# Global attention computes its scores twice, the second time keys-first, so that the probabilities are never transposed

## The chip, the cores and the metric

The kernel runs on one core of one Trainium2 chip. The metric is the device time of one launch in microseconds; of several runs the median is taken. The core has the engines TensorE (matmuls; the profile calls it PE, and its weight loads PEld), VectorE (DVE), ScalarE (ACT), GpSimd (POOL) and SyncE (SP), which here issues the DMAs.

## The reference

One layer of a hybrid backbone over 1024 latent tokens and 256 context tokens, width 1024: a modulated norm, three token mixers side by side (windowed attention, global attention, a bidirectional recurrence), their gated merge, and a gated feed-forward network. The change concerns the global attention alone. Eight query heads of 64 share two key heads; each query reads all 256 + 1024 keys:

```python
def dense_attn(q, k, v, sink=None):
    ...
    s = jnp.einsum('bqkgd,bjkd->bkgqj', q.reshape(B_, Lq, KV, G, hd), k).astype(jnp.float32) * hd ** -0.5
    ...
    p = jax.nn.softmax(s, axis=-1)[..., :k.shape[1]].astype(v.dtype)
    return jnp.einsum('bkgqj,bjkd->bqkgd', p, v).reshape(B_, Lq, HQ * hd)

def global_attn(q, k, v, ck, cv):
    ...
    k_all = jnp.concatenate([ck, k], axis=1)
    v_all = jnp.concatenate([cv, v], axis=1)
    qb = jnp.moveaxis(q.reshape(B_, nb, BLOCK, HQ, hd), 1, 0)
    o = lax.map(lambda qblk: dense_attn(qblk, k_all, v_all), qb)
```

Everything is float32. The queries and keys of this branch are normalised with large gains, so the scores need their maximum taken away before the exponential.

## The kernel before

The kernel goes through its stages in order: modulation and context, the recurrence (about 90 to 430 us of the profile), token-major projections of both attentions, windowed attention (`br` 0), global attention (`br` 1, about 889 to 1221 us), merge, output projection, feed-forward network. Most products are made from split operands: each operand is rounded into a high part (type `F32R`), the rest is kept as a low part, and a product is two or three passes of `F32R` matmuls.

A framework orders the instructions of each engine ahead of time from dependences, priorities and its own cost model, places the semaphores, and gives out buffers. The order of the program text, which is the priority, comes from `weave`: it draws from several generators in turn, in proportion to given weights. In the attention stages three are woven: the scores of iteration `it + 1`, the values of iteration `it`, and filler, which is the gate projection (`gate_unit`: eight steps of three matmuls 512 wide for one accumulator). 32 filler steps (`FILL0`) run beside the preparation, the other 80 of the global stage over 15 of its 16 iterations. An iteration is one tile of 128 tokens and one group of four heads (`it` = 2 x tile + group).

Before the change both attentions run through `attention`. `prep` loads keys and values two blocks of 128 at a time, splits them, and transposes the keys into `KH` (the high part, twice, one copy under the other: 128 rows) and `KL` (the low part, twice). `qprep` loads, scales and splits the queries and transposes them into `QT`, whose 128 rows are the high part (64) and the low part (64) of one head. So one matmul with `KH` gives high x high plus low x high, and one with `KL` the rest.

`softmax_global` (L1415 on) makes, with `QT` of one head as the stationary operand, the scores of 128 queries by 256 context keys for four heads at once (`sbc`), and by 1024 latent keys for one head at a time (`sbl`, two halves of 512). VectorE takes the maxima straight from the accumulator banks, ScalarE makes the exponentials with the maximum as its bias and sums them (`pc`, `plat`). The probabilities lie with queries on the partitions. `values` (L1303 on) turns them, four 128 x 128 transposes for each of the ten key blocks (`pp`, L1321), ScalarE rounds the result to `ph` (L1325), VectorE subtracts to `pl` (L1326), and two matmuls with the values `VHL` (64 high and 64 low columns) as stationary operand accumulate the transposed output `po` for all four heads, 512 wide (L1307, L1308). The value matmuls follow their transposes by two blocks (`PV_LAG`). The reciprocal sums are spread by GpSimd (L1450), turned by TensorE (`pr`, L1316) and multiplied in at the end (L1343).

The accumulator memory has eight banks: tag `mm` gives two buffers of two banks, `a` and `b` two buffers of one bank each.

## Time and profile before

| what | value |
|---|---|
| median of 3 runs | 2128.88 us (2126.53 to 2129.55) |
| span of the profiled execution, the only time that the page gives of it | 2127.9 us |
| TensorE matmul, busy | 2085.8 us, 98% |
| TensorE weight load, busy | 1743.1 us, 82% |
| VectorE, busy | 1380.5 us, 65% |
| ScalarE, busy | 1001.2 us, 47% |
| GpSimd, busy | 288.1 us, 14% |
| mean granted TensorE clock | 0.998 |
| DMA, mean over the span | 108 GB/s |

Busy times are unions of an engine's instructions. In the groups of the profile a row has the line, the engine, the operation, what it writes and reads (for a matmul: result, streamed operand, stationary operand), the shape, the count, the busy time, the mean of one in ns, and the idle time before with what ended it. In the timeline a row begins with the start and the duration in us. The ends of matmuls are modelled by the profiler, so neighbouring matmuls seem to overlap, and what one takes is read from start to start.

### The profile page before, as it was taken

What the parts mean: (1) busy time and instruction counts of PE and PEld (TensorE: products, weight loads), DVE (VectorE), ACT (ScalarE), POOL (GpSimd) and SP (SyncE); (2) the same over time, 40 slices, a digit from 0 to 9 for tenths busy, and PEclk for the clock granted to TensorE, in tenths of its full rate; (3) what the DMA queues carried; (4) which work ended last, traced back from release to release, by engine and by line L of the source; (5) the groups of instructions that cost most, each with busy time, mean ns of one, the idle gap of its engine ahead of it and who ended that gap; (6) DMA issues with size and microseconds to landing.
All of it is one profiled execution on the core that took longest, in us unless ns stands there. A gap on an engine that the chain in (4) does not pass through costs nothing.

```text
span 2127.9 us, 30555 instructions
## 1 busy us (share of the span) xinstructions
PE 2085.8 (98%) x11686; PEld 1743.1 (82%) x11686; DVE 1380.5 (65%) x2299; ACT 1001.2 (47%) x1761; POOL 288.1 (14%) x257
## 2 busy tenths in 40 slices
PE   7999999999999999999999999999999999999997
PEld 4888888888988888878888788888888888888887
DVE  4736756636665777678887746569777777664423
ACT  4333333311123777678888734346445544453222
POOL 0000000010021222100000000011333344100111
PEclk9999999999999999999999999999999999999999
DMA  9511111136543211211100354641222222285342
GB/s 359 207 44 36 46 50 41 46 113 214 186 137 123 78 59 41 80 55 35 35 28 28 115 200 142 194 156 55 99 79 89 80 80 88 81 287 201 109 126 86
DMA packets 95490, 229.28 MB, mean 108 GB/s; under 512 B 10736, under 2 KB 35824, under 8 KB 94320
## 3 DMA queue, kind: packets, MB, share of 16 engines
q1 hardware_dynamic: 95344, 227.33, 32.1%
q8 instruction: 92, 1.51, 0.3%
q14 instruction: 54, 0.44, 0.1%
HBM read 181.68 MB, written 45.61 MB: 107 GB/s over the span
## 4 chain that ended last, share of the span: by engine, by line
PE 69%; DVE 3%; ACT 2%; issue 1%; DMA 1%; POOL 1%; SPq 0%; DVEq 0%; ACTq 0%; POOLq 0%
PE pp L1321 4%; PE gz L199 3%; PE dn L929 3%; PE dn L928 3%; PE dn L930 3%; PE gz L200 3%; PE gz L201 3%; PE up L852 2%; PE up L853 2%; PE up L854 2%; PE po L1307 2%; PE po L1308 2%; PE br L200 2%; PE br L201 2%; PE br L199 2%; PE upd L853 2%
## 5 line engine op out<-in xcount | busy, mean ns | idle before, releaser
L175 ACT CAST wh<-wr 128x1024 fp32r<-128x1024 f32 (+1 forms) x139 | 145.1, 1044 | 398.7 <-PE dn L929 69.1
L176 DVE TENSOR_TENSOR wl<-wr,wh 128x1024 fp32r<-128x1024 f32 (+1 forms) x139 | 171.1, 1232 | 221.1 <-ACT wh L175 206.7
L1326 DVE TENSOR_TENSOR pl<-pp,ph 128x512 fp32r<-128x512 f32 x236 | 159.3, 687 | 29.2 <-ACT ph L1325 23.5
L199 PE MATMUL gz<-hh,wh 128*128 128x512 f32 x384 | 156.3, 408 | 3.1 <-ACT gs L523 3.1
L1325 ACT CAST ph<-pp 128x512 fp32r<-128x512 f32 x236 | 135.7, 587 | 37.4 <-PE pp L1321 35.3
L201 PE MATMUL gz<-hh,wl 128*128 128x512 f32 x384 | 152.3, 397 | 0.0
L200 PE MATMUL gz<-hl,wh 128*128 128x512 f32 x384 | 152.1, 396 | 0.0
L210 PE MATMUL tm<-wl,hh 128*128 128x256 f32 x384 | 108.9, 283 | 3.3 <-DVE wl L176 3.3
L209 PE MATMUL tm<-wh,hh 128*128 128x256 f32 x384 | 108.9, 284 | 0.9 <-ACT qo L615 0.9
L211 PE MATMUL tm<-wh,hl 128*128 128x256 f32 x384 | 108.6, 283 | 0.0
L1307 PE MATMUL po<-ph,VHL 128*128 128x512 f32 x236 | 106.1, 450 | 1.4 <-ACT ph L1325 1.0
L929 PE MATMUL dn<-ac,wh 128*128 128x512 f32 x256 | 99.7, 390 | 0.0
L930 PE MATMUL dn<-ac,wl 128*128 128x512 f32 x256 | 99.6, 389 | 0.0
L928 PE MATMUL dn<-ac,wh 128*128 128x512 f32 x256 | 99.6, 390 | 0.0
L1308 PE MATMUL po<-pl,VHL 128*128 128x512 f32 x236 | 97.1, 411 | 0.1
L199 PEld LDWEIGHTS gz<-hh,wh 128*128 128x128 f32 x384 | 72.7, 189 | 17.2 <-ACT gs L523 5.2
L201 PEld LDWEIGHTS gz<-hh,wl 128*128 128x128 f32 x384 | 72.5, 189 | 15.0
L200 PEld LDWEIGHTS gz<-hl,wh 128*128 128x128 f32 x384 | 72.8, 190 | 11.6
L210 PEld LDWEIGHTS tm<-wl,hh 128*128 128x128 f32 x384 | 73.7, 192 | 4.3 <-DVE wl L176 4.0
L1321 PE MATMUL pp<-ident,plat 128*128 128x128 f32 x512 | 76.6, 273 | 0.0
L1321 PEld LDWEIGHTS pp<-ident,plat 128*128 128x128 f32 x512 | 62.7, 140 | 16.9 <-DVE pl L1326 1.2
L199 PE MATMUL br<-yh,wh 128*128 128x512 f32 x192 | 74.3, 390 | 1.6 <-ACT yh L1468 1.6
(1420 smaller groups left out, 5898.7 us busy)
## 6 DMA issues: line engine op xcount, KB each, us to landing
wr<-in_w_cm SPq DMA_DIRECT2D x48, 512.0 KB, 3.7
wr<-in_w_up SPq DMA_DIRECT2D x44, 512.0 KB, 3.5
wr<-in_w_down SPq DMA_DIRECT2D x33, 512.0 KB, 3.5
wmr<-in_w_mod SPq DMA_DIRECT2D x32, 512.0 KB, 4.5
gate_d<-gs SPq DMA_DIRECT2D x48, 256.0 KB, 2.3
sgt<-gate_d SPq DMA_DIRECT2D x24, 512.0 KB, 3.4
act_d<-u SPq DMA_DIRECT2D x22, 512.0 KB, 2.6
st<-act_d SPq DMA_DIRECT2D x44, 256.0 KB, 4.5
```

Source lines behind the costliest of these rows:

```text
L175: A.copy(hi[:, :n], raw[:, :n])
L176: (lo_eng or V).tensor_tensor(out=lo[:, :n], in0=raw[:, :n], in1=hi[:, :n].bitcast(F32), op=ALU.subtract)
L199: T.matmul(psl, wh[:, k, c], hh[:, k0 + k, cols], start=s, stop=False)
L200: T.matmul(psl, wh[:, k, c], hl[:, k0 + k, cols], start=False, stop=False)
L201: T.matmul(psl, wl[:, k, c], hh[:, k0 + k, cols], start=False, stop=e)
L210: T.matmul(psl, hh[:, k, toks], wl[:, k % 4, :], start=False, stop=False)
L928: T.matmul(z, w[0][:, c], h[0], start=s, stop=False)
L929: T.matmul(z, w[0][:, c], h[1], start=False, stop=False)
L930: T.matmul(z, w[1][:, c], h[0], start=False, stop=e)
L1307: T.matmul(po, vv, ph, start=n == 0, stop=False)
L1321: T.transpose(pp[:, h], PT(h, n), ident)
L1326: V.tensor_tensor(out=pl, in0=pp, in1=ph.bitcast(F32), op=ALU.subtract)
```

## The change

The second branch gets a function of its own, `attention_t`. In an iteration it does the following.

- `maxima` (for `it + 1`): the scores as before, but with `KH` alone, one pass instead of two, only for their maximum over keys. The exponential needs no exact maximum, since the same number is taken away from every key of a query.
- The maximum of each query, split in two parts, goes into two extra columns of the query's high part (`QM`), which is turned once more into `Q2`. The rows under the low part of the keys in `KL` hold ones in those two places and zeros elsewhere, so the matmul of `KL` with `Q2` adds the low part of the score and takes away the maximum at once.
- `values`: for two key blocks at a time, transposed scores: a key block is the stationary operand, the queries of four heads are streamed (512 wide), one pass with `KH` and `Q1`, one with `KL` and `Q2`. ScalarE makes the exponential `e`, ScalarE (even steps) or GpSimd (odd steps) rounds it to `ph`, VectorE subtracts to `pl`; all are 128 x 1024. The value matmuls have `ph` or `pl` of one head and key block as stationary operand and stream `VX`: 64 low columns, 64 high columns and two columns of which the first ones gather the sum (130 for `ph`; 66, without the low columns, for `pl`). They follow by one step of two blocks (`PT_LAG`), with three buffers of `ph` and `pl`.
- The output lies with queries on the partitions; the two parts are added, scaled by the reciprocal of the gathered sum, and turned by two transposes, which are issued in the next iteration (`late`, `flush`).
- The output takes two banks of tag `b`, one for two heads; the filler's accumulator takes tag `a` in this branch.

```diff
-                gen = gate_units(ap_, units, "b")
-                attention(tc, nc, ap_, br, ins, kv_d[br], q_d[br], y_d, mm2, bank, ident, identr, gen, nf)
+                gen = gate_units(ap_, units, "ba"[br])
+                if br == 0:
+                    attention(tc, nc, ap_, br, ins, kv_d[br], q_d[br], y_d, mm2, bank, ident, identr, gen, nf)
+                else:
+                    attention_t(tc, nc, ap_, br, kv_d[br], q_d[br], y_d, mm2, bank, ident, identr, gen, nf)
...
+    def maxima(it):
+        tt, g = divmod(it, 2)
+        st = tl([P, 5, 4], "st", f"{it}")
+        sc = mm2(f"sbc{it}").rearrange("p a (b c) -> p (a b) c", b=2)
+        for h in range(4):
+            T.matmul(sc[:, h], Q1[it][:, h], KH[:, g, :256], start=True, stop=True)
+        V.tensor_reduce(out=st[:, 0], in_=sc, axis=AX.X, op=ALU.max, negate=True)
+        yield
+        for h in range(4):
+            s2 = mm2(f"sbl{it}{h}")
+            for hf in range(2):
+                k = 256 + hf * 512
+                T.matmul(s2[:, hf], Q1[it][:, h], KH[:, g, k:k + 512], start=True, stop=True)
+            V.tensor_reduce(out=st[:, 1, h:h + 1], in_=s2.rearrange("p a b -> p (a b)"), axis=AX.X, op=ALU.max,
+                            negate=True)
+            if h < 3:
+                yield
+        m = st[:, 2]
+        V.tensor_tensor(out=m, in0=st[:, 0], in1=st[:, 1], op=ALU.min)
+        qm = QM[it % 3]
+        V.tensor_copy(qm[:, :, HD], m)
+        V.tensor_tensor(out=qm[:, :, HD + 1], in0=m, in1=qm[:, :, HD].bitcast(F32), op=ALU.subtract)
+        Q2[it] = turn(qm, f"M{it}")
+        yield
...
+        def pv(n, ph, pl):
+            for j in range(2):
+                k = 2 * n + j
+                parts = [(ph, 0), (pl, HD)]
+                for e, (p, o) in enumerate(parts if k < NK - 1 else parts[::-1]):
+                    for h in range(4):
+                        T.matmul(po[h // 2][:, h % 2, o:], p[:, j, h * P:(h + 1) * P], VX[:, k, g, o:], ...)
...
+        for n in range(NK // 2):
+            s2 = mm2(f"st{it}{n}")
+            for j in range(2):
+                c = slice((2 * n + j) * P, (2 * n + j + 1) * P)
+                T.matmul(s2[:, j], KH[:, g, c], q1, start=True, stop=False)
+                T.matmul(s2[:, j], KL[:, g, c], q2, start=False, stop=True)
+            ph = tl([P, 2, 512], "ph", f"{it}{n}", PT_BUF, F32R)
+            pl = tl([P, 2, 512], "pl", f"{it}{n}", PT_BUF, F32R)
+            e = tl([P, 2, 512], "e", f"{it}{n}")
+            A.activation(e, s2, AF.Exp)
+            if n % 2:
+                G.tensor_copy(ph, e)
+            else:
+                A.copy(ph, e)
+            V.tensor_tensor(out=pl, in0=e, in1=ph.bitcast(F32), op=ALU.subtract)
+            prev.append((n, ph, pl))
+            if len(prev) > PT_LAG:
+                pv(*prev.pop(0))
+            yield
...
+        weave((maxima(it + 1), 6) if it + 1 < n_it else (None, 0), (main(), NK // 2 + 2), (some(fill_gen, b - a), b - a))
```

The preparation of keys, values and queries is as before but for the pads, the buffers (`kv` has one instead of two), and the copy of each query's high part into `QM` by GpSimd. The parts of `attention` that only the global branch used are taken out.

## The prediction

> **What bounds the kernel now.** I read the page, then the stage of the change in stretches (global attention runs from about 889 to 1221 us), then its matmuls one by one by their start times, because the ends of matmuls are modelled and starts are not.

> ```profile
> span 2127.9 us, 30555 instructions
> PE 2085.8 (98%) x11686; PEld 1743.1 (82%) x11686; DVE 1380.5 (65%) x2299; ACT 1001.2 (47%) x1761; POOL 288.1 (14%) x257
> ```
> ```profile
> core 0: us, PE busy (x) PEld busy (x) DVE busy (x) ACT busy (x) POOL busy (x), PEclk, DMA share, GB/s
> 929.00:1190.00 261.00, 259.59 (x1512) 213.62 (x1511) 212.08 (x353) 214.34 (x462) 5.63 (x14) 1.00 0.10 32
> 889.00:929.00 40.00, 38.35 (x211) 30.55 (x210) 20.60 (x40) 28.23 (x62) 0.40 (x1) 1.00 0.31 95
> 1190.00:1226.00 36.00, 32.85 (x169) 25.45 (x168) 25.89 (x39) 26.59 (x45) 0.40 (x1) 1.00 0.53 176
> ```
> In the steady part TensorE is busy 259.59 of 261 us; VectorE and ScalarE have 212 and 214, about 82% each, and the DMA engines a tenth. So TensorE's own list of work sets the end, and a microsecond taken from ScalarE is worth nothing here. The two edges leave TensorE 1.65 and 3.15 us idle.

> One GpSimd copy is made per iteration, so it gives the period:

> ```profile
> L1450 POOL COPY yT_r__9139<-st__8989 x1: 401/401/401, 938.7 to 938.7; 128x256 f32<-128x256 f32 x1
> L1450 POOL COPY yT_r__11914<-st__11768 x1: 403/403/403, 1180.1 to 1180.1; 128x256 f32<-128x256 f32 x1
> ```
> 13 iterations lie between: (1180.1 - 938.7) / 13 = 18.57 us. There are 16 (8 token tiles by 2 groups).

> Prices on TensorE, from start to start:

> ```profile
> 1191.15 0.60 PE L1321 MATMUL pp<-ident,plat 128*128 128x128 f32 x4
> 1191.50 0.48 PE L1307 MATMUL po<-ph,VHL 128*128 128x512 f32 x1
> 1191.82 0.39 PE L1308 MATMUL po<-pl,VHL 128*128 128x512 f32 x1
> ...
> 1193.64 0.39 PE L1435 MATMUL sbl<-KH,QT 128*128 128x512 f32 x1
> 1193.87 0.40 PE L1436 MATMUL sbl<-KL,QT 128*128 128x512 f32 x1
> 1194.11 0.39 PE L1435 MATMUL sbl<-KH,QT 128*128 128x512 f32 x1
> ```
> ```profile
> 1050.12 0.46 PE L1286 MATMUL pq<-identr,qs_q 128*128 128x128 f32 x4
> 1050.58 0.50 PE L1307 MATMUL po<-ph,VHL 128*128 128x512 f32 x1
> ...
> 1051.04 0.28 PE L1426 MATMUL sbc__10488<-KL,QT 128*128 128x256 f32 x1
> 1051.16 0.28 PE L1425 MATMUL sbc__10488<-KH,QT 128*128 128x256 f32 x1
> ...
> 1055.23 0.68 PE L1316 MATMUL pr<-ident,yT_r__10421 128*128 128x128 f32 x4
> 1055.67 0.48 PE L1308 MATMUL po<-pl,VHL 128*128 128x512 f32 x1
> 1055.98 0.40 PE L200 MATMUL gz<-hl,wh 128*128 128x512 f32 x1
> ```
> A 512-wide matmul takes 0.23 us, a 256-wide one 0.12. Four transposes and one wide matmul take 1191.82 - 1191.15 = 0.67, so a transpose is (0.67 - 0.23) / 4 = 0.11. The `pr` pair likewise is 0.75 - 0.23 = 0.52, a turn of Q (`pq`, four) 0.46.

> Check of the prices on one iteration: scores 8 x 0.12 + 16 x 0.23 = 4.64; 40 transposes 4.40; values 20 x 0.23 = 4.60; `pr` 0.52; `pq` 0.46; gate filler 80 steps over 15 iterations, three wide matmuls a step, 5.33 x 0.69 = 3.68. Sum 18.30, measured 18.57. The prices hold, with 0.27 us over.

> **The change part by part, on TensorE.** All other operations are weighed below.

> Gone per iteration: the second score pass (4 x 0.12 + 8 x 0.23 = 2.32), the 40 transposes (4.40), the 20 wide value matmuls (4.60), `pr` (0.52). Together 11.84.

> Added: transposed scores, 10 key blocks by two 512-wide passes, 4.60; a second turn of Q that carries the maxima, 0.46; two transposes of the result, 0.22. That is 5.28, all with rows.

> Added, and the term that decides: the values. The probabilities are now the stationary operand, so each of 10 key blocks, 2 parts and 4 heads loads its own 128 x 128 weights and then streams only 130 or 66 columns: 80 loads and 80 narrow matmuls. The nearest rows are at the kernel's very end, where the down projection does the same with rounded operands and 128 columns:

> ```profile
> 2105.76 0.22 PE L928 MATMUL dl<-ac,wh 128*128 128x128 f32 x1
> 2105.82 0.27 PE L929 MATMUL dl<-ac,wh 128*128 128x128 f32 x1
> 2105.94 0.27 PE L930 MATMUL dl<-ac,wl 128*128 128x128 f32 x1
> ...
> 2108.28 0.28 PE L930 MATMUL dl<-ac,wl 128*128 128x128 f32 x1
> ```
> ```profile
> 1191.47 0.19 PEld L1307 LDWEIGHTS po<-ph,VHL 128*128 128x128 f32 x1
> 1191.58 0.19 PEld L1308 LDWEIGHTS po<-pl,VHL 128*128 128x128 f32 x1
> ```
> From 2105.82 to 2108.28 there are 22 intervals: 0.112 us each. The first interval, 2105.76 to 2105.82, is 0.06: that matmul followed a wide one, under which its weights were loaded. So streaming 128 columns takes about 0.06 and the load about 0.11; the loads set the pace. The second fence shows the same: after transposes a load starts at 1191.47 and the next one only 0.11 later, when the first has left the way free. Therefore I price the 66-wide matmuls like the 130-wide: 80 x 0.112 = 8.96 us. Ends: 80 x 0.06 = 4.80 if every load were hidden; upward the trace gives nothing over 0.12 (the 256-wide row), 9.60.

> [...] The trace's 0.112 decides for these operands.

> Sum per iteration: -11.84 + 5.28 + 8.96 = +2.40 us, so 20.97; times 16 is +38.4 us.

> **Beside TensorE.**

> ```profile
> L1326 DVE TENSOR_TENSOR pl<-pp,ph 128x512 fp32r<-128x512 f32 x142 | 95.7, 688 | 18.6 <-ACT ph L1325 14.1
> L1325 ACT CAST ph<-pp 128x512 fp32r<-128x512 f32 x142 | 81.6, 588 | 14.8 <-PE pp L1321 13.2
> L1439 DVE TENSOR_REDUCE st__10271<-sbl 128x1 f32<-128x1024 f32 x4 | 4.9, 1216 | 0.1
> L1442 ACT ACTIVATE plat<-sbl,st__10271 128x1024 f32<-128x1024 f32 x4 | 4.5, 1122 | 0.3 <-DVE st__10271 L1440 0.2
> L176 DVE TENSOR_TENSOR wl<-wr,wh 128x1024 fp32r<-128x1024 f32 x5 | 6.1, 1223 | 2.9 <-ACT wh L175 2.9
> L175 ACT CAST wh<-wr 128x1024 fp32r<-128x1024 f32 x4 | 4.3, 1072 | 0.0
> ```
> ScalarE: ten casts of 512 (5.9), four exponentials of 1024 and four of 256, and the copy `pc` go; five exponentials of 1024 (5 x 1.12 = 5.6) and three casts of 1024 (3.2, priced by `wh`) come, with about 2 us of small copies. It falls by some 4 us. VectorE: ten subtractions at 0.69 (6.9) become five at 1.22 (6.1); the five reductions stay (6.1). It stays near 15 us. GpSimd gets two copies of 128 x 1024, from its 256-wide row about 4 x 0.40 = 1.6 us each, and the small pads and copies into `QM`. All of it has less work than TensorE's 20.97, so it costs nothing by volume; the cover is TensorE's list itself. It can still cost by order: the values wait only one step (`PT_LAG` = 1), see the second rival.

> Edges: the maxima of iteration 0 need five reductions, a turn, then a transposed score, exponential, cast and subtraction before the first value matmul; iteration 1's maxima and gate filler partly cover that. In the last iteration no maxima are left as cover, but the branch lift already fills there. Before, the edges lost 4.8 us; I take 4 more, bounds 0 and 12. `kv` has one buffer instead of two in the five preparations; 32 filler steps (22 us) stand beside them, priced at nothing. The queue of SyncE issues the same loads and stores; the store of `yT` moves into the next iteration, and nothing reads that tensor before the third branch of the merge. The gates' accumulators move to the banks `a`, since two output banks `b` are now held per iteration; a turn may wait there for a bank, which the scheduler fills with other matmuls.

> Sum: 2127.9 + 38.4 + 4 = 2170.3. The page gives the span as the only time of the profiled execution; the median of the runs, 2128.88, is 1.0 above it, so 2171.

> **The rivals.**

> Narrow matmuls hide their loads (the other side). If pairs run at p us, the values cost 80p; the iteration gains nothing at 80p = 6.56, p = 0.082, and below that the change is faster. At 0.06 throughout: 4.80, so 1.76 us less an iteration, 28 us, 2105 with the edges. For it: the 0.06 interval shows that streaming is not the limit. Against: the other 22 intervals, which are this very pattern. [...]

> The step's chain is longer than the step. A value matmul needs exponential 1.12, cast 1.07 (or the GpSimd copy, about 1.6) and subtraction 1.22, one after the other, with hand-overs of about 0.1 and perhaps a reduction of 1.22 in front: 3.8 to 5.4 us. A step of TensorE lasts 20.97 / 5 = 4.19. If two steps of an iteration wait 0.6 each, it is 16 x 1.2 = 19 us more, 2190; if every step took 4.9, the iteration is 24.5 and the time about 2227. For it: TensorE's order is fixed ahead and the lag is one step. Against: now the same kind of chain costs under 0.3 us an iteration, though with a lag of two.

> ScalarE was the hidden bound, and its relief pays. At 214 of 261 us against 259.59 on TensorE the profile leaves no room; it would give about 2125.

> **How the numbers follow.** The load-paced case has 0.70: 2171, its own range 2155 to 2185. The chain that is too long has 0.18: 2185 to 2227. Hidden loads have 0.09 (faster 0.06, within 0.2% 0.03), ScalarE or another unseen gain 0.03, mostly faster. 0.2%, 4 us, is about what a measurement of this kernel can tell from no change. So faster 0.08, same 0.04, slower 0.88. For 8 in 10 the range reaches from 2148 (a term smaller by 1.4 us an iteration, or an edge that costs nothing and better order) to 2205 (half of the second rival).

> **What would show it.** In the profile after: the starts of the value matmuls 0.11 apart in runs of 16, and loads busier than before in that stage; iterations 20.5 to 21.5 us apart; ScalarE's share there down from 82% to near 60%; TensorE still over 95% busy. Starts nearer 0.06 in the 66-wide half make me wrong downward; TensorE idle in front of value matmuls, ended by VectorE's subtraction, upward.

## The result

The changed kernel takes 2216.57 us (median of 4 runs, 2215.93 to 2221.6), the kernel before 2127.7 beside it; the ratio is 1.042 with a 95% interval of 1.0403 to 1.0436. I had forecast 2171 and a range up to 2205: slower, as forecast, but by 89 us instead of 43. The page after:

```profile
span 2214.1 us, 31061 instructions
PE 2148.9 (97%) x12166; PEld 1814.9 (82%) x12166; DVE 1365.2 (62%) x2201; ACT 935.0 (42%) x1475; POOL 329.9 (15%) x307
```
VectorE and ScalarE have less to do than before, TensorE 63 us more. At the end of windowed attention the two traces still agree within 3 us; the first matmul of the branch lift (`br`, after global attention) starts 85 us later, and from the output projection on every matmul is 86 us later. All of the loss is in the stage that was changed.

The turn of the maxima (`pq1M`) comes once an iteration, so its start cuts the stage into iterations. Stretches between such starts, with the busy time of each engine, the granted clock, the DMA share and GB/s:

```profile
992.30:1018.60 26.30, 25.53 (x141) 22.84 (x141) 15.20 (x20) 12.18 (x17) 2.49 (x3) 0.81 0.12 41
1018.60:1040.60 22.00, 20.95 (x137) 18.36 (x137) 13.69 (x19) 10.81 (x16) 2.62 (x3) 1.00 0.08 25
1040.60:1063.60 23.00, 21.43 (x137) 18.60 (x137) 13.77 (x19) 10.20 (x14) 2.62 (x3) 1.00 0.04 12
1063.60:1089.10 25.50, 24.41 (x140) 21.56 (x140) 15.11 (x20) 12.03 (x17) 2.62 (x3) 0.87 0.14 42
...
926.60:1269.20 342.60, 324.21 (x2028) 283.33 (x2027) 209.15 (x281) 161.34 (x217) 39.15 (x43) 0.97 0.08 25
```
The last row holds 15 iterations: 342.60 / 15 = 22.84 us each, against 18.57 before and 20.97 forecast. Two things stand in these rows that were not in the sum. TensorE is idle for 1.0 to 1.6 us of each undisturbed iteration (22.00 - 20.95), where before it was idle 0.1. And in some iterations the granted clock is 0.81 or 0.87; those last 25.5 and 26.3 us.

What the idle time waits for, in the same 342.60 us (total, times, longest):

```profile
engine line waited for: us in total, times, longest us
PE pq1M L1452 <- DVE QM L1493: 13.7, 15, 1.2
PE po L1508 <- DVE pl L1527: 4.4, 15, 0.3
```
Most of it is the turn of the maxima waiting for VectorE. One such place, TensorE first, then VectorE:

```profile
1061.84 0.39 PE L1518 MATMUL st<-M,KL 128*128 128x512 f32 x1
1062.07 0.33 PE L1508 MATMUL po<-VX,ph 128*128 128x130 f32 x2
1063.60 0.54 PE L1452 MATMUL pq1M<-identr,QM 128*128 128x128 f32 x4 [1.21 <-DVE QM L1493]
...
1065.53 0.63 PE L201 MATMUL gz<-hh,wh 128*128 128x512 f32 x1
1065.96 0.63 PE L202 MATMUL gz<-hl,wh 128*128 128x512 f32 x1
1066.39 0.63 PE L203 MATMUL gz<-hh,wl 128*128 128x512 f32 x1
```
```profile
1060.58 1.23 DVE L1527 TENSOR_TENSOR pl<-e,ph 128x1024 fp32r<-128x1024 f32 x1 [1.29 <-POOL ph L1524]
1061.73 1.22 DVE L1485 TENSOR_REDUCE st<-sbl 128x1 f32<-128x1024 f32 x1
1062.98 0.16 DVE L1490 TENSOR_TENSOR st<-st 128x4 f32<-128x4 f32 x1
1063.18 0.17 DVE L1492 CAST QM<-st 128x4 fp32r<-128x4 f32 x1
1063.38 0.17 DVE L1493 TENSOR_TENSOR QM<-st,QM 128x4 fp32r<-128x4 f32 x1
```
The last reduction stands behind a subtraction of 1.23 us, and three small operations follow. TensorE's order has the turn only two value matmuls after the scores, so TensorE stands, though value matmuls that are ready (the late turn, below, puts them first) come right behind it. The first fence also shows the clock: from 1065.53 a 512-wide matmul takes 0.43 us from start to start instead of 0.23.

```profile
1058.87:1062.28 3.41, 3.41 (x22) 3.02 (x21) 2.12 (x3) 0.59 (x2) 1.04 (x1) 1.00 0.00 0
1062.28:1065.70 3.42, 2.21 (x21) 2.10 (x20) 1.17 (x4) 2.53 (x3) 0.40 (x1) 1.00 0.00 0
1065.70:1069.10 3.40, 3.40 (x15) 3.11 (x14) 2.45 (x2) 1.54 (x3) 0.00 (x0) 0.50 0.03 11
1069.10:1072.50 3.40, 3.40 (x17) 3.21 (x17) 1.81 (x6) 1.44 (x4) 0.00 (x0) 0.50 0.73 220
1072.50:1075.90 3.40, 3.40 (x19) 2.60 (x17) 1.51 (x3) 2.71 (x3) 0.00 (x0) 1.00 0.15 39
```
The box with the stop is followed by two boxes at clock 0.50. Over the stage (881 to 1305 us) the trace grants half clock for 54.6 us, of which 23.9 lie in the 342.60 us above and 30.7 at the two edges; before there was none in this stage. At half clock a 512-wide matmul takes 0.43 us instead of 0.23, and eight narrow ones from 1067.56 to 1069.23, 0.21 each instead of 0.11. So half clock costs about half its length, an estimate of 27 us.

The entrance has a stop of its own, the first transpose of the keys (waits from 884 to 926 us):

```profile
PE kt10h L1446 <- ACT kk_h L1438: 6.0, 1, 6.0
```
There is filler to put here, but its accumulator now takes tag `a`, and the two key transposes that wait hold both buffers of that tag.

### The profile page after: what moved, and what is told of

It reads as the page before. It is cut to its first block, busy times and chain, and to the rows that moved or that the text cites. A ratio compares the mean times of both kernels' runs of the same rounds, so it can differ in the third digit from the quotient of the medians.

```text
span 2214.1 us, 31061 instructions
## 1 busy us (share of the span) xinstructions
PE 2148.9 (97%) x12166; PEld 1814.9 (82%) x12166; DVE 1365.2 (62%) x2201; ACT 935.0 (42%) x1475; POOL 329.9 (15%) x307
## 4 chain that ended last, share of the span: by engine, by line
PE 65%; DVE 5%; ACT 4%; POOL 1%; issue 1%; DMA 1%; SPq 0%; DVEq 0%; POOLq 0%; ACTq 0%
PE po L1508 5%; PE dn L934 3%; PE dn L933 3%; PE dn L935 3%; PE gz L201 2%; PE gz L202 2%; PE up L857 2%; PE up L858 2%; PE up L859 2%; PE gz L203 2%; PE br L203 2%; PE br L202 2%; PE br L201 2%; DVE pl L1527 2%; PE upd L857 2%; PE upc L857 2%
## 5 line engine op out<-in xcount | busy, mean ns | idle before, releaser
L1527 DVE TENSOR_TENSOR pl<-e,ph 128x1024 fp32r<-128x1024 f32 x80 | 97.8, 1224 | 107.3 <-ACT ph L1526 86.7
L1522 ACT ACTIVATE e<-st 128x1024 f32<-128x1024 f32 x80 | 81.9, 1025 | 121.8 <-PE st L1518 121.6
L1508 PE MATMUL po<-VX,ph 128*128 128x130 f32 x640 | 103.2, 283 | 0.6 <-ACT ph L1526 0.6
L1508 PEld LDWEIGHTS po<-VX,ph 128*128 128x128 f32 x640 | 94.2, 199 | 10.7 <-ACT ph L1526 4.7
L1508 PE MATMUL po<-VX,pl 128*128 128x66 f32 x640 | 97.9, 280 | 5.0 <-DVE pl L1527 4.9
L1508 PEld LDWEIGHTS po<-VX,pl 128*128 128x128 f32 x640 | 88.2, 201 | 10.6 <-DVE pl L1527 10.1
L1485 DVE TENSOR_REDUCE st<-sbl 128x1 f32<-128x1024 f32 x64 | 77.6, 1219 | 9.6 <-PE sbl L1484 9.5
L1524 POOL CAST ph<-e 128x1024 fp32r<-128x1024 f32 x32 | 36.0, 1125 | 277.7 <-ACT e L1522 277.7
```

The costliest lines, as they stand in the source:

```text
L1508: T.matmul(po[h // 2][:, h % 2, o:], p[:, j, h * P:(h + 1) * P], VX[:, k, g, o:], start=k == 0 and e == 0 and h % 2 == 0, stop=k == NK - 1 ...
L1527: V.tensor_tensor(out=pl, in0=e, in1=ph.bitcast(F32), op=ALU.subtract)
```

## The experiments

The theory after the comparison: TensorE's list is as long as forecast, and the rest is an order that makes TensorE stand (the turn of the maxima, the entrance) and half clock, which follows boxes in which the array streams few columns. Rivals: the narrow value matmuls cost more than their price; the stops alone bring the half clock; the step's chain (exponential, cast, subtraction) sets the pace. The experiments stand here by subject; the expectations count them in the order of the runs, so their fourth is the one with GpSimd's running sum and their eighth the one without it.

**The turn one stretch later.** An extra `yield` puts the turn of the maxima one piece of interleaved work further on.

```
         V.tensor_tensor(out=qm[:, :, HD + 1], ...)
+        yield
         Q2[it] = turn(qm, f"M{it}")
```

> Edit: the turn of the maxima is written one step later, so that TensorE gets the last value matmuls in front of it. Nothing is left out. In the changed kernel TensorE stood still in front of that turn 15 times, 13.7 us in all, and four half-clock stretches of the steady part (946, 994, 1066 and 1270 us, 34 us long together) each began within 3.4 us of such a stop. Theory A (a 3.4 us window in which TensorE streams too few columns halves the clock; the narrow value matmuls bring it near the limit and the stop takes it below): the stops go (-14 us) and with them the half-clock stretches of the steady part (34 us at half clock lose 17 us); about 2186, 2178 to 2200. Theory B (the narrow matmuls alone halve the clock): only the stops go, the stretches stay; about 2203. Theory C (the stop moves to the next place, the transposed scores that need the turned maxima): no change, 2216.

Measured: 2192.13 us (2190.4 to 2197.5), ratio 1.0302 (1.0285 to 1.0319). The waits over its 15 steady iterations, and the stretch itself:

```profile
PE po L1509 <- DVE pl L1528: 7.3, 28, 0.3
PE pq1Q L1452 <- ACT gs L525: 0.2, 1, 0.2
```
```profile
926.80:1250.50 323.70, 316.12 (x2045) 275.16 (x2045) 209.05 (x282) 163.06 (x219) 44.12 (x43) 1.00 0.08 27
```
One `yield` gives back 24 us. The turn no longer waits, half clock in the steady part is gone (clock 1.00), and an iteration lasts 323.70 / 15 = 21.58 us. That is within what the theory said (2178 to 2200) and more than the stops alone (13.7 us) could give, although the waits for the subtraction grew from 4.4 to 7.3 us.

**Wider streams, the stop left in.** The value matmuls stream 256 and 192 columns instead of 130 and 66; the extra columns are not read. The stationary side, its loads and the stop of the turn stay.

```
-T.matmul(po[h // 2][:, h % 2, o:], p[...], VX[:, k, g, o:], ...)
+T.matmul(po[h // 2][:, h % 2, o:], p[...], flat[:, (2 * k + g) * VW + o:(2 * k + g) * VW + 256], ...)
```

> Edit: each value matmul streams on past its columns, 256 wide for the high part and 192 wide for the low part instead of 130 and 66; the surplus lands in unused columns of the same bank, and nothing is left out. The number of weight loads is the same. If the load sets the pace (0.112 us), the price rises to at most 0.12 us for half of them: 0 to +6 us. If the streaming set the pace, the price would double: +80 us or more. On the clock: theory A (too few columns streamed in a window) expects the half-clock stretches of the steady part to vanish, although TensorE still stops for the turn of the maxima: -17 us, so about 2200 to 2207 in sum. Theory D (standing still alone halves the clock, whatever is streamed): the stretches stay, 2216 to 2223.

Measured: 2198.24 us (2196.01 to 2199.65), ratio 1.0322 (1.0307 to 1.0338). Waits over its steady part, and one box of the clock's grid with a stop in it:

```profile
PE pq1M L1457 <- DVE QM L1498: 9.6, 14, 0.9
PE po L1513 <- DVE pl L1532: 0.3, 2, 0.2
```
```profile
1054.58:1057.99 3.41, 2.53 (x20) 2.45 (x21) 1.11 (x5) 2.17 (x3) 0.40 (x1) 1.00 0.00 0
1057.99:1061.40 3.41, 3.26 (x27) 3.00 (x26) 2.69 (x6) 2.59 (x6) 0.00 (x0) 1.00 0.21 77
```
The stops are still there, yet no box of the steady part is at half clock (granted clock 1.00 from 926.6 to 1257 us). So standing alone didn't bring it here; what changed is how much is streamed. The stops are shorter here (9.6 us in all, the longest 0.9), which may be why the time lies just under the 2200 to 2207 expected; but their length didn't decide on the clock. In the changed kernel a stop of 0.77 us (box from 942.82) was followed by half clock, and stops of 1.10 and 1.20 us (boxes from 1130.55 and 1198.82) were not: 2,974 columns were streamed in the first box, 4,356 and 3,974 in the other two. And 80 matmuls with twice to three times the columns make no iteration longer (21.78 us with 0.64 of stop in it, against 21.58 with 0.49 of waits for the late turn); the median start is 0.120 us after the one before with 256 columns, 0.111 with 192. The load set the pace here, as priced.

**Filler on the other buffers at the entrance.** The first two filler units take tag `b`.

```
-                yield from gate_unit(pool, n, i, mode)
+                yield from gate_unit(pool, n, i, "b" if u < 2 else mode)
```

> Edit: the first two units of the gate filler, which run beside the preparation of keys and values, accumulate in tag b again, as before the change; the others stay in tag a. Theory: in the preparation the filler could not start because the key transposes hold both buffers of tag a; TensorE stood still 6.0 us before the first of them and ran at half clock for 6.8 us after it. Expected: the filler fills that stop, -6 us and -3 us of half clock, about 2207. Rival: the stop is a late load or cast and stays; 2216.

Measured: 2212.34 us (2207.38 to 2222.3), ratio 1.0395 (1.0367 to 1.0424). The 6.0 us stop is gone and the first turn starts 8.2 us earlier (918.4 instead of 926.6), but only about 4 of the 9 us expected arrive at the end, and the two intervals overlap: iterations of 23.15 us, with more half clock than the changed kernel has (34.1 against 23.9 us). A shift by some us moves the iterations against the clock's grid; that this brings the additional half clock is my reading, which no run separates. Alone this edit is nearly worthless.

**All three edits.**

> The first three edits together: the turn of the maxima one stretch of filler later, value matmuls that stream 256 and 192 columns, the first two filler units on the other buffers. Theory A (the turn's stops, the entrance's stop and the half clock are separate and add up): the late turn alone gave 2192.1, of which about 6 us is the entrance's stop and 3 to 7 us half clock that is left, so 2176 to 2188, with no half clock in the steady part and iterations of 21.5 to 21.8 us. Rival E (the edits overlap, since each only takes away half clock): 2190 or above. Rival F (wider streams cost the array's time once it no longer stands): 2198 or above, iterations of 22 us and more.

Measured: 2182.77 us (2179.17 to 2184.6), ratio 1.026 (1.0244 to 1.0275), iterations of 21.32 us, and no half clock between the first turn and the last but for the rest of a stretch that began ahead of the first turn. The edits add up; the rivals with 2190 and above fall. The iteration is 0.2 shorter than expected.

**A step more of lag, with the late turn.** `PT_LAG` = 2, buffers as before.

> The late turn, and the value matmuls of a step issued two steps after its probabilities instead of one, with three buffers as before. Theory A (what is left of idle on TensorE, 28 waits of 7.3 us for the low part's subtraction, is the step's chain being a little longer than the step): 2183 to 2188 against 2192.1 of the late turn alone, and those waits gone. Rival G (with three buffers and two steps of lag the casts wait for the value matmuls that free them, and the scores for the casts): 2192 or slower, with ScalarE and GpSimd waiting for TensorE. Rival H (the subtraction of the last step is what ends late, and lag doesn't reach it): 2190 to 2194, waits still there.

Measured: 2190.99 us (2188.76 to 2193.46), ratio 1.0301 (1.0285 to 1.0316). In time, nothing (2183 to 2188 was expected); in the trace, much. The waits for the subtraction are gone and an iteration lasts 20.88 us, 0.70 less than with the late turn alone. But half clock is back, three boxes in the steady part and 30.7 us at the edges instead of 13.7. Four boxes of its grid:

```profile
988.45:991.86 3.41, 3.41 (x33) 3.41 (x32) 2.09 (x2) 1.66 (x3) 0.82 (x1) 1.00 0.30 91
991.86:995.27 3.41, 3.41 (x15) 3.08 (x15) 2.58 (x7) 1.44 (x4) 0.00 (x0) 0.50 0.38 139
1073.78:1077.19 3.41, 3.41 (x34) 3.41 (x33) 0.33 (x2) 0.63 (x3) 0.43 (x1) 1.00 0.00 0
1077.19:1080.61 3.42, 3.42 (x12) 2.84 (x12) 2.46 (x7) 1.60 (x4) 0.00 (x0) 0.50 0.00 0
```
Here TensorE is busy all 3.41 us, with matmuls and with loads, and the next box is at half clock all the same. It holds 33 or 34 matmuls, nearly all narrow. A full "busy" was no protection here.

**All three edits and the lag.**

> The three edits together (late turn, wider value streams, filler on the other buffers at the entrance) and the lag of two steps. Theory A (in the steady part of the three edits only 0.2 us of idle is left, so lag has nothing to take away there): 2178 to 2184, against 2182.8. Rival M (the edges, where 5 us are waited for exponentials and casts, gain from the lag): 2172 to 2178.

Measured: 2183.33 us (2180.15 to 2185.98), ratio 1.0253 (1.0238 to 1.0268), the same as without the lag. The iteration is 20.86 us instead of 21.32. The time lies in the range of theory A by luck: its reason (nothing left to take away) was wrong, since the waits of the loads are a row of their own. With one step of lag (first fence) and two (second), in the steady part:

```profile
PEld po L1514 <- DVE pl L1533: 7.8, 29, 0.5
PEld po L1514 <- ACT ph L1532: 4.5, 14, 0.4
```
```profile
PEld sbl L1489 <- ACT e L1528: 4.8, 15, 0.4
```
The 7 us won are lost at the end of the stage, where the last iteration has nothing to put beside two more steps of values: TensorE waits 6.0 us for the output's scaling and 2.6 for a cast.

**Without the low part's value matmuls.** With the late turn; 40 of 80 narrow matmuls left out.

```
-                parts = [(ph, 0), (pl, HD)]
+                parts = [(ph, 0)]
```

> The late turn, and the 40 value matmuls of the low part of the probabilities left out (its subtraction still runs, its share of the values is missing in the output). Theory A (TensorE's list sets the pace, and each of these narrow matmuls costs a load of 0.11 us): 40 x 0.110 x 16 = 70 us less, and the 7 us of waits for the subtraction: 2192.1 - 77 = 2115, range 2108 to 2126. Rival I (the chain from scores over exponential and cast to the value matmuls sets the pace): the time falls by less than 40 us, to above 2150, with TensorE waiting for ScalarE or GpSimd.

Measured: 2130.5 us (2125.81 to 2134.49), ratio 1.001 (1.0 to 1.0019). It is 61.6 us less than the late turn alone; 77 were expected, and 2130.5 is just outside the range. An iteration lasts 17.97 us, with 15.5 us of waits over 15 of them, 12.6 of these for VectorE's reductions and again for the maxima. Corrected for the waits on both sides, (21.58 - 0.49) - (17.97 - 1.03) = 4.15 us for 40 matmuls, 0.104 each. The list sets the pace, and the price per matmul holds; the chain is close behind.

**The values as the loaded side.** The other way to use probabilities that lie keys-first: load the values and stream the probabilities, 20 matmuls of 512 columns. The output then lies transposed, as before the change, and the sums over keys have to be made apart. First, with a running sum on GpSimd (and the filler's accumulator on tag `b` again):

```
+                T.matmul(po, vv, ph[:, j], start=k == 0, stop=False)
+                T.matmul(po, vv, pl[:, j], start=False, stop=k == NK - 1)
...
+                G.tensor_tensor(out=acc, in0=acc, in1=e, op=ALU.add)
```

> Edit: the values become the stationary operand again (20 matmuls 512 wide per iteration instead of 80 narrow ones); the probabilities still come keys-first and are never transposed. The sums over keys are gathered by GpSimd from the exponentials, summed over the partitions by eight narrow matmul records with unrounded data, and multiplied in through two unrounded turns, an iteration later; the filler accumulates in tag b throughout; ScalarE makes all five casts. Nothing is left out. Theory (loads of the narrow matmuls are the main loss): per iteration -9.0 + 4.6 + 0.9 + 0.5 - 0.2 = -3.2 us, 51 us in all, and no half-clock stretch (-25), and no stop in the preparation (-6): about 2135, 2120 to 2155. Rival: the order of the steps with its short lag is the main loss, whatever the values cost; then TensorE waits instead, and the time stays above 2180.

Measured: 2209.05 us (2206.78 to 2209.99), ratio 1.0372 (1.0357 to 1.0388), far from the 2135 expected. Groups of four iterations, the two longest waits, and a moment of VectorE and GpSimd:

```profile
L1521 POOL TENSOR_TENSOR acc<-acc,e 128x1024 f32<-128x1024 f32 x16 | 40.2, 2515 | 16.6 <-ACT e L1518 16.3
L1524 DVE TENSOR_TENSOR pl<-e,ph 128x1024 fp32r<-128x1024 f32 x20 | 33.9, 1712 | 0.0
```
```profile
PE po L1505 <- DVE pl L1524: 20.4, 25, 2.6
PE pq1M L1450 <- DVE QM L1491: 15.0, 8, 2.0
```
```profile
1100.07 2.46 POOL L1521 TENSOR_TENSOR acc<-acc,e 128x1024 f32<-128x1024 f32 x1 [1.38 <-ACT e L1518]
...
1100.20 2.35 DVE L1488 TENSOR_TENSOR st<-st 128x4 f32<-128x4 f32 x1
```
The last fence is the plainest: a minimum over 4 elements takes VectorE 2.35 us, and ends within 0.02 us of GpSimd's addition beside it; alone it takes 0.16. The subtraction takes 1.71 in the mean instead of 1.22. So this run said nothing of the wide form. Its steady part is at half clock for 41 us, too: wide matmuls didn't keep the clock up where the stops were long (up to 2.6 us).

**The same without the sum.** The running sum is left out (only one step's probabilities reach the normaliser), the turn is late, and casts are shared as in the changed kernel. The filler stays on tag `b`.

> The probabilities keys-first, but with the values as the loaded side: 20 value matmuls of 512 columns in place of 80 narrow ones, the turn of the maxima late, casts shared by ScalarE and GpSimd as in the changed kernel. The running sum of the probabilities on GpSimd is left out (the normaliser of the output comes from one step's probabilities plus one), so that nothing with two inputs from memory runs beside VectorE's subtraction. Theory A (80 loads of 0.11 us are what keys-first costs; VectorE's subtraction was slowed in the fourth experiment by GpSimd's additions): per iteration 21.58 - 0.46 - 9.03 + 20 x 0.23 + about 0.8 for the turns of the sums = 17.5, so 2192.1 - 65 = 2127, range 2112 to 2145, and the subtraction back at 1.2 us mean. Rival J (the wide form waits for the subtraction whatever runs beside it, since 4 wide matmuls of a step give it less cover than 16 narrow ones): 2170 or above with the subtraction at 1.2 us.

Measured: 2127.01 us (2124.67 to 2129.43), ratio 0.9999 (0.9989 to 1.0008); 2127 was expected. The subtraction is back at 1.22, and no box in the stage is at half clock (the row covers about five iterations):

```profile
L1526 DVE TENSOR_TENSOR pl<-e,ph 128x1024 fp32r<-128x1024 f32 x24 | 29.1, 1222 | 4.2 <-ACT ph L1523 3.3 <-POOL ph L1521 0.5
```
The iteration is 18.25 us, against 21.58 with the narrow form and the late turn. That the total fits so well is luck in part: the iteration was to be 17.5 us, and what it is longer comes back at the edges, where this kernel has no half clock and no stop of 6 us at the entrance. The lag is still one step, so rival J falls, and the short lag isn't the main loss either. So, without the running sum, the rest of the change is level with the kernel before, and of the 65 us that separate it from the late turn, 53 lie in the iterations, where the narrow value matmuls are what differs most.

**A complete version of it.** GpSimd adds only the two halves of a step (512 columns), and five matmuls with a side of ones sum over the keys; then the same with two steps of lag.

> The complete computation with the values as the loaded side: GpSimd adds the two halves of each step's exponentials (512 columns, rounded to the matmul's format), and 5 wide matmuls with a side of ones sum them over the keys, in place of the eighth experiment's 8 short sums and 4 turns. Theory A: against the eighth experiment 12 short items of about 0.1 us go (1.3) and 5 x 0.23 = 1.15 come, so iterations of 18.0 to 18.3 us and 2118 to 2132, the same as the kernel before. Rival K (GpSimd's additions, though half as long as in the fourth experiment, slow VectorE's subtraction and the value matmuls wait for it): the subtraction above 1.4 us mean, several us of waits for it, 2140 or above.

> The kernel with the sides of ones, and the value matmuls two steps behind. Theory A (waits for a step's chain are hidden by a step more of lag): the waits for subtraction and casts gone and 3 to 8 us less than with one step of lag, 2113 to 2126. Rival L (the buffers of three steps hold back the casts): no gain or slower, with the scores waiting for ScalarE.

Measured: 2201.7 us (2199.93 to 2204.06), ratio 1.0341 (1.0325 to 1.0356), and 2201.27 (2196.33 to 2205.54), ratio 1.033 (1.0312 to 1.0348). The rival K holds, with the subtraction at 1.58 us and 7.2 us of waits for it; but three times as much, 21.7 us, is waited for GpSimd's sum itself, which it didn't name. The lag doesn't help. In the first of the two (groups of four iterations; waits of the stage):

```profile
L1529 DVE TENSOR_TENSOR pl<-e,ph 128x1024 fp32r<-128x1024 f32 x20 | 31.4, 1580 | 1.7 <-POOL ph L1524 0.9 <-ACT ph L1526 0.7
L1528 POOL TENSOR_TENSOR es<-e 128x512 fp32r<-128x512 f32 x20 | 28.0, 1398 | 31.1 <-ACT e L1522 31.1
```
```profile
PE ps L1505 <- POOL es L1528: 21.7, 45, 1.0
PE po L1510 <- DVE pl L1529: 7.2, 13, 2.5
```
No complete form of the change that I ran beats the kernel before; the best is 2.5% behind it.

## Why the prediction was wrong

The terms, per iteration and as measured:

| step of the prediction | forecast | measured |
|---|---|---|
| 80 narrow value matmuls | 8.96 us | 9.03 (starts 0.116 apart with 130 columns, 0.110 with 66) |
| transposed scores | 4.60 us | 4.72 |
| iteration of TensorE's list | 20.97 us | 20.88 and 20.86, where the waits are taken out by the late turn and the lag; less the half clock in them (10.2 and 3.2 us in 15 iterations) an estimate of 20.5 and 20.8 |
| the turn's place in the order | nothing | 13.7 us in 15 iterations |
| waits for the subtraction | 0.18 chance of 1.2 an iteration | 4.4 us in 15 iterations |
| the clock | not in the sum | 23.9 us at half clock in the steady part, about 12 us lost |
| edges | +4 us, 0 to 12 | +17.9 |

**What held.** The deciding term, the load-paced price of 0.112, is right to 1%. Runs of four at full clock, one row each:

```profile
1084.19 0.64 PE L1508 MATMUL po<-VX,pl 128*128 128x66 f32 x4
1084.65 0.64 PE L1508 MATMUL po<-VX,ph 128*128 128x130 f32 x4
1085.13 0.58 PE L1508 MATMUL po<-VX,pl 128*128 128x66 f32 x4
1085.55 0.47 PE L201 MATMUL gz<-hh,wh 128*128 128x512 f32 x1
```
1085.55 - 1084.19 is 1.36 us for 12, 0.113 each. The rival of hidden loads falls with that, and with the wider streams, which make no iteration longer. ScalarE's relief paid nothing; its share of the stage is 47% (161.34 of 342.60), not the 60% I gave. TensorE is 97% busy over the page, but 94.6% in the 15 iterations (324.21 of 342.60), and the loads are hardly busier there (83%) than before (82%). My own sign for upward, TensorE idle in front of value matmuls for the subtraction, is there with 4.4 us; the greater part of the idle time, 13.7 us, stands in front of the turn, where no sign of mine pointed.

**First failing step: the clock was not in the sum.** The prediction names the granted clock nowhere, though the rows it quoted had the column. I took 1.00 as given, because TensorE would stay busy. The narrow matmuls stream 66 or 130 columns in 0.112 us, against 512 in 0.23, while the profile calls them busy; in three places a box of them with a stop in it (0.77 us in the box from 942.82, 1.21 in those from 990.60 and 1062.28) was followed by half clock. It is 12 us of the steady part. At the edges another 30.7 us are at half clock, at most 15 lost.

**Second: the turn of the maxima, priced by its work (0.46) and covered by "the scheduler fills with other matmuls".** I named the wait for a bank, and not the wait for VectorE's last reduction and the three operations behind it. The cover existed, but the order didn't use it. The late turn shows it: the turn's wait gone, 24 us less in all, clock included.

**Third: the edges.** The key transposes were counted as covered by filler, "priced at nothing", though the same paragraph moves that filler onto the two buffers which the transposes hold: 6.0 us idle. The edge that I bounded with 12 came to 17.9 (86.2 of span less 16 x 4.27).

The second rival, the chain longer than the step, was there, but small: 0.29 us an iteration, not 1.2.

Do these make up the difference? 16 iterations: list 38.4 (as forecast), the turn 14.6, the subtraction 4.7, half clock 12.7, together 70.4; measured 16 x (22.84 - 18.57) = 68.3, 2 us less. With the edges 86.2, the whole difference of the spans. How the 17.9 us at the edges divide between stops and half clock wasn't separated: the two overlap at the entrance.

**The half clock** is told best by the columns that TensorE streams in a box of 3.41 us. Over the 13 kernels (before, after and 11 experiments), between 925 and 1250 us, for boxes at full clock (worked out from the start and width of every matmul; a few records are missing in each trace, so single cases may be misplaced):

| columns in the box | boxes | next box at half clock |
|---|---|---|
| under 2,400 | 12 | 11 |
| 2,400 to 2,800 | 7 | 6 |
| 2,800 to 2,950 | 5 | 2 |
| 2,950 to 3,600 | 37 | 6 |
| above 3,600 | 1139 | 0 |

512-wide matmuls at 0.23 us would stream 7,600. In these boxes the limit lies between a third and a half of that. The length of the stops doesn't tell it: a stop of 0.77 us was followed by half clock, stops of 1.10 and 1.20 us were not, and with two steps of lag it came without any stop. That the columns are the cause is shown in one direction, by the wider streams, which took the half clock away with the stops left in; where exactly the limit lies is only read off these boxes.

## What to carry to other kernels

A matmul that turns its loaded side over, 128 columns loaded for 66 or 130 streamed, was paid at the load in these runs (starts 0.116 us apart with 130 columns, 0.110 with 66); count loads before products when you choose which operand lies still. Then look at the clock column: in a stretch of such matmuls stops of 13.7 us came with 23.9 us at half clock, and moving the turn gave back 24 us: a stop there can be paid twice, so place wide work between them and keep every wait (a turn of something just reduced, above all) one piece of work behind its producer. Price a moved step by where the order puts it, not by its own duration.

## What the runs showed of the hardware

Half clock followed a box of 3.41 us in which TensorE's matmuls and loads were busy without a gap (33 matmuls, nearly all narrow, from 988.45 us in the run with two steps of lag). I had taken a busy share of 100% as safe.

In the run with GpSimd's running sum, VectorE operations with two inputs from memory lasted longer beside GpSimd's additions, which have two as well: a minimum over 4 elements took 2.35 us instead of 0.16 and ended within 0.02 us of the addition, and the subtraction took 1.71 in the mean instead of 1.22. A reduction out of the accumulator banks that began 0.77 us before such an addition ended (1097.92) took 1.23, as elsewhere. In the changed kernel the same is seen the other way, and with GpSimd's casts. There 14 of the 75 subtractions from 926 to 1269 us overlap a cast that begins after them, and it is the cast that lasts longer, 1.16 to 2.01 us instead of 1.04:

```profile
932.00 1.22 DVE L1527 TENSOR_TENSOR pl<-e,ph 128x1024 fp32r<-128x1024 f32 x1
932.11 2.01 POOL L1524 CAST ph<-e 128x1024 fp32r<-128x1024 f32 x1 [4.42 <-ACT e L1522]
```
The cast ends 0.90 us after the subtraction, and the other 13 do so within 0.02. With the late turn a subtraction of the weights (`wl`) that begins 0.29 us before a running cast ends takes 1.36 us instead of 1.22. What the two engines share, so that one stands, is not shown by these rows.
